# Moving the token tiles of a three-pass matmul within SBUF, with another order of its passes

## The chip, the core and the metric

One core of a Trainium2 chip runs the whole program. The metric is the device time of one execution in microseconds; the kernel before took 1469.27 us (median of 3 runs, 1468.96 to 1470.71).

## The reference

One layer of a decoder for a prompt of 4096 tokens (width 1024) and a sample batch of 64 new tokens. All arithmetic is float32.

```python
h = rmsnorm(x, g_pre)
z = h @ w_in                        # 1024 -> 2816 columns, split among three head groups
out_a = silu(cg) * cb * conv3(cc * ch)                  # gated short convolution, 256 channels
out_b = silu(ag) * window_attention(q, k, v, sink)      # window 128, 8 q heads, 2 kv heads, head dim 64
out_c = silu(mg) * cross_attention(mq, mem_k, mem_v)    # 4 heads, 256 memory tokens
y = concat(out_a, out_b, out_c) @ w_out
out = x + rmsnorm(y, g_post)
```

Beside the two outputs the kernel returns the last keys, values and convolution rows, and the keys and values of the memory.

## The kernel before, in words

**Three passes for float32.** TensorE multiplies float32r operands in one pass. To keep float32 precision each operand is split in two, hi (a rounded copy, made by ScalarE) and lo (the rest, made by VectorE), and a product is hi x hi + hi x lo + lo x hi. In the input projection the weights are the operand that is loaded into the array (128 columns at a time) and the tokens are the operand that is streamed (260 columns at a time).

**The input projection.** The tokens are 8 blocks of 2 x 260 columns, and the 1024 rows of the contraction are two halves of 4 slices (KH) of 128. A weight tile of one product is 128 partitions x 2 x 512: hi and lo of 4 slices x 128 columns. `product` (line 378, its matmul on line 383) runs one product into a PSUM bank: for each slice k the three matmuls (w hi, t hi), (w hi, t lo), (w lo, t hi), twelve in all. Two column blocks of z and two token halves make a 2 x 2 block product, done with 7 products instead of 8 (Strassen's scheme in Winograd's form): `PRODUCTS` names the weight sums (A11 to S4) and the token sums (B11 to T4). Three passes over column groups (`PHASES`: 4, 4 and 3 pairs of column blocks) go through all blocks; within a block the steps p = 0 to 6 take one entry of `PRODUCTS` each, and a step runs that product for its 4 (or 3) pairs q. The first two blocks of the first pass are plain 8-product blocks (`plain_block`), since the weight sums are not there yet. That is 64 + 168 + 224 + 168 = 624 products.

**Token tiles.** Each step needs one hi and one lo tile [128, 4, 260]; `split` (or `x_split` in the plain blocks) makes the next step's while this step's products run. The pool `hp` has two places for hi and two for lo, so steps take the places in turn. Below `hp` on the left stack of SBUF lie the constants, the pool `tiny` for small sums, `wa` with 21 weight tiles, `place` and the pool `hx` of four float32 token tiles; above it lie the z tiles and temporary rows. The fourth pair's weights lie in `wb`, at the right end of SBUF. The weight tiles are reused later for w_out and the split mix of the attention.

**Attention and output projection.** Small pieces of the memory products and of the first attention groups run inside the third pass. Then 32 blocks of 128 tokens follow, one after the other; each runs the output projection of its block (line 1662, 512 streamed columns) between the scores and values of later blocks. `open_attention` lays the pools of this part on the left stack from the end of `place` on, with three unused tiles (gap0, gap1, gap2) between them. Softmax of the cross attention keeps maximum (mx), scaled maximum (nm), sum (den) and reciprocal (rd) in four small tiles with a tag each, three places a tag. The sample batch's attention is done in pieces in blocks 26 to 30 and uses the same tags.

**Order.** The instruction order of TensorE, VectorE, ScalarE, GpSimd and SyncE is the written one in the plain blocks and in the third pass up to the end, and a scheduler's elsewhere. Jobs of VectorE and ScalarE are spread by hand behind the products of each step.

Of the kernel before, what the change touches and what calls it, by code (L numbers as in the profile page):

```python
# [8 lines left out]
F32 = mybir.dt.float32  # L9
F32R = mybir.dt.float32r  # L10
# [5 lines left out]
P = 128  # L16
D = 1024
KT = D // P
KH = KT // 2
# [2 lines left out]
NB = 8  # L22
NT = 4096 + NS
HW = 260
NBLK = NT // (2 * HW)
CT = 256
NCH = 4096 // CT
# [19 lines left out]
def f(ap):  # L47
    return ap.bitcast(F32)
# [3 lines left out]
def hybrid_layer(ctx: ExitStack, tc: tile.TileContext, a: dict):  # L52
# [10 lines left out]
    class InOrder:  # L63
# [6 lines left out]
        def __getattr__(self, name):  # L70
# [4 lines left out]
    V, TE, S, G = (InOrder(engine) for engine in (nc.vector, nc.tensor, nc.scalar, nc.gpsimd))  # L75

    const = ctx.enter_context(tc.tile_pool(name="const", bufs=1))
    tiny = ctx.enter_context(tc.tile_pool(name="tiny", bufs=3))
# [8 lines left out]
    mhalf = const.tile([P, 8], F32, name="mhalf")  # L87
# [5 lines left out]

    diag = const.tile([P, 2 * HW], F32, name="mix_s")
    mix_s = diag[:, : 8 * NS].rearrange("p (k n) -> p k n", n=NS)

    rowd = [tc.dram_tile([2 * HW], F32, name=f"rowd{b}") for b in range(NBLK)]
    hd = [{o: tc.dram_tile([P, KH, HW], F32, name=f"hd{b}_{o}") for o in ("B12", *(o for _, o in PRODUCTS))}
          for b in range(NBLK)]
    sd = {}  # L100
# [9 lines left out]
    pa = ExitStack()  # L110
# [3 lines left out]

    place = ctx.enter_context(tc.tile_pool(name="place", bufs=1)).tile([P, 2, KH, HW], F32, name="place")
    hxp = pa.enter_context(tc.tile_pool(name="hx", bufs=4))
    hp = pa.enter_context(tc.tile_pool(name="hp", bufs=2))
    own = ExitStack()
    kept_z = ExitStack()
    zp, used = {}, {1: [], 2: []}  # L120
# [41 lines left out]
    def z_tile(w, name):  # L162

        pool = zp[w].pop(0)
        used[w].append(pool)
        return pool.tile([P, w, 2, HW], F32, tag="z", name=name)

    def z_done(order):

        for w in zp:  # L170
            zp[w] += [used[w][i] for i in order if i < len(used[w])]
            used[w] = []

    late, late_rows = [], []

# [9 lines left out]
    def store(dst, src):  # L185
        if store_queue[0] is G:
            G.dma_start(dst, src)  # L187
        else:
            late.append(lambda: DMA.dma_start(dst, src))

    def temp(name):
        return tp.tile([P, 2 * HW if 1 in zp else 2 + 2 * HW], F32, tag="t", name=name)
# [80 lines left out]
    def row_load(j):  # L273
        if j < 5 * NBLK:
            g = RG * j - NS
# [11 lines left out]
    def row_step():  # L287

        j = sq[0]
        if j == 5 * NBLK:  # L290
            return
# [48 lines left out]
    def gain_of(o, k):  # L340
        kk = KH * (int(o[1]) - 1) + k
        return gpre[:, kk : kk + 1]
# [25 lines left out]
            store(hd[b][o], ops[o])  # L368

    def split(src, name):  # L370
        hi = hp.tile([P, KH, HW], F32R, tag="hi", name=f"hi{name}")
        lo = hp.tile([P, KH, HW], F32R, tag="lo", name=f"lo{name}")
        S.copy(hi, src)
        V.tensor_tensor(lo, src, f(hi), op=ALU.subtract)
        return hi, lo


    def product(w, h, bank, first=True, last=True):
        i = 0
        for k in range(KH):  # L380
            ks = slice(k * P, (k + 1) * P)
            for l, r in ((w[:, 0, ks], h[0][:, k]), (w[:, 0, ks], h[1][:, k]), (w[:, 1, ks], h[0][:, k])):
                TE.matmul(bank[:, :HW], l, r, start=first and i == 0, stop=last and i == 3 * KH - 1)  # L383
                i += 1

    def evict(p, banks, z1, z2):
# [27 lines left out]
    def finish_parts(b, z, idx, zsi):  # L414

        z = flat(z)
        if b == 0:
            S.copy(zs[:, zsi, :], z[:, :NS])
        if idx == 0 and b == NBLK - 1:
            kl = temp("kl")  # L420
# [9 lines left out]
    def finish_v(b, z):  # L430
        t = temp(f"v{b}")[:, : 2 * HW]
        S.copy(t, flat(z))
        if b == 0:
            S.copy(zs[:, 5, :], t[:, :NS])
        if b == NBLK - 1:
            store(a["o_vp"], t[:, 2 * HW - P :])
# [86 lines left out]
    ws = {}  # L523
# [69 lines left out]
    raw0, zz, pending, h0, kept = {}, {}, {}, {}, {}  # L593

    def x_split(b, o, meanwhile=lambda: None):
        x = xs[0, b][o]
        h0[b, o] = hi, lo = [hp.tile([P, KH, HW], F32R, tag=n, name=f"{n}0_{b}{o}") for n in ("hi", "lo")]
        for k in range(KH):
            if k == 1:
                meanwhile()  # L600
            g = gain_of(o, k)
            S.mul(hi[:, k], x[:, k], g)
            V.scalar_tensor_tensor(lo[:, k], x[:, k], g, f(hi[:, k]), op0=ALU.mult, op1=ALU.subtract)
# [82 lines left out]
    def plain_block(b):  # L686
        banks, zz[b] = {}, [[None, None], [None, None]]
        for s, (wo_, ho, tag) in enumerate(PLAIN):
            flush()
            plain_loads(b, s)  # L690
            jobs, done, adds = plain_jobs(b, s), 0, s % 4 > 1
            row, half = 1 - s % 2, s // 4
            for q in range(4):
                if q % 2 == 0 and not adds:
                    banks[q // 2, tag] = accumulator("xy".index(tag), 2, f"c0_{b}_{q}_{s}")
                product(ws[0, q, wo_], h0[b, ho], banks[q // 2, tag][:, q % 2], not adds, adds)
                if adds and q % 2:
                    if half == 0:
                        zz[b][q // 2][row] = z_tile(2, f"z0_{b}_{q}_{row}")
                    S.copy(zz[b][q // 2][row][:, :, half], banks[q // 2, tag][:, :, :HW])  # L700
                upto = len(jobs) * (q + 1) // 4
                for fn in jobs[done:upto]:
                    fn()
                done = upto
        z_done((0, 1, 2, 3))
# [9 lines left out]
    written_order()  # L715
    x_of(0, 0, "B11", 2)
    first_w("A21")
    S.mul(tiny.tile([P, 8], F32, tag="mx", name="table"), mhalf, 1.0)
    first_w("A11", 0, 1)
    x_of(0, 0, "B21")  # L720

# [244 lines left out]
    last = NBLK - 1  # L966
# [118 lines left out]
    def open_attention():  # L1085

        nonlocal ps, mixp, wp, wl, kp, bq, yp, yq, sp
        own.close()
        psa.close()
        pa.close()  # L1090

        ps = {tag: ctx.enter_context(tc.tile_pool(name=f"ps{tag}", bufs=1, space=bass.MemoryType.PSUM)) for tag in (*range(4), "pv", 4, 5)}
        left = lambda name, bufs=1: att.enter_context(tc.tile_pool(name=name, bufs=bufs))
        bq, kp, third["sm"] = left("bq"), left("kp"), left("sm")
        left("gap0").tile([P, 128], F32, name="gap0")
        yq, mixp, yp0 = left("yq"), left("mixp"), left("yp0")
        left("gap1").tile([P, 64], F32, name="gap1")
        third["skc"], third["sqb"], yp1, wd0 = left("skc"), left("sqb"), left("yp1"), left("wd0")
        left("gap2").tile([P, 48], F32, name="gap2")
        yp = yp0, yp1  # L1100
        sp, wl, wd1 = left("sp"), left("wl"), left("wd1")
        wp = wd0, wd1
# [80 lines left out]
    class Group:  # L1183
# [125 lines left out]
            self.cross_exps(s, hh)  # L1309

        def cross_max(self, s, hh):
            mx, nm, den, rd = (tiny.tile([P, 4], F32, tag=t, name=f"x{t}{self.b}_{hh}")[:, :2] for t in ("mx", "nm", "den", "rd"))
            V.tensor_reduce(mx, s, axis=AX.X, op=ALU.max)
            V.tensor_scalar(nm, mx, -SCALE, None, op0=ALU.mult)
            self.cross_sums[hh] = den, rd, nm
# [156 lines left out]
    def sample_mem(bh):  # L1472
# [6 lines left out]
        p, on, pt = (big[:, i] for i in (8, 9, 10))  # L1479
# [5 lines left out]
        for j in range(2):  # L1485
            for hh in range(2):
                r = slice(hh * 64, hh * 64 + 64)
# [8 lines left out]
        s = psum(3, f"sms{bh}")[:, :256]  # L1496
        for b in range(nb):
            for j in range(2):
                TE.matmul(s[32 * b : 32 * b + 32, :], qb[:, j, b, :], km[:, j, b, :], start=j == 0, stop=j == 1,
                          tile_position=(0, 32 * b))  # L1500
        mx, nm, den, rd = (tiny.tile([P, 4], F32, tag=n, name=f"sm{n}{bh}") for n in ("mx", "nm", "den", "rd"))
        V.tensor_reduce(mx[:, 0:1], s, axis=AX.X, op=ALU.max)
        V.tensor_scalar(nm[:, 0:1], mx[:, 0:1], -SCALE, None, op0=ALU.mult)
        S.activation(p, s, AF.Exp, bias=nm[:, 0:1], scale=SCALE, accum_out=den[:, 0:1])
# [6 lines left out]
        o = psum(2, f"smo{bh}")[:, :256]  # L1511
# [7 lines left out]
        t = psum(3, f"smot{bh}")  # L1519
# [3 lines left out]
        for j in range(2):  # L1523
            for hh in range(2):
                r = slice(hh * 64, hh * 64 + 64)
# [6 lines left out]
    def sample_window():  # L1532
# [6 lines left out]
        for j in range(4):  # L1539
            for kvh in range(2):  # L1540
                r = slice(kvh * 64, kvh * 64 + 64)
# [15 lines left out]
        sm = [sms[i // 2][:, i % 2] for i in range(4)]  # L1557
        for half in range(2):
            s = psum(1 + half, f"sws{half}")
            s3 = s.rearrange("p (h k) -> p h k", h=2)  # L1560
            for i in range(2):
                pr = 2 * half + i
                for b2 in range(2):
                    TE.matmul(s3[b2 * 64 : b2 * 64 + 64, i, 0:P], qb[:, 2 * pr + b2, :], kc[:, 2 * pr + b2, :],
                              start=True, stop=True, tile_position=(0, 64 * b2))
                TE.matmul(s3[:, i, P:192], qb[:, 2 * pr : 2 * pr + 2, :].rearrange("p b c -> p (b c)"), zs[:, 4, :],
                          start=True, stop=True)
            S.copy(sms[half], s3[:, :, 0:192])
        mx = tiny.tile([P, 4], F32, tag="mx", name="swmx")
        for half in range(2):  # L1570
            V.copy_predicated(sms[half], msk[:, 2 * half : 2 * half + 2], neg)
            V.tensor_reduce(mx[:, 2 * half : 2 * half + 2], sms[half], axis=AX.X, op=ALU.max)
        nm = tiny.tile([P, 4], F32, tag="nm", name="swnm")
        V.tensor_scalar(nm, mx, -SCALE, scol[:, 1:2], op0=ALU.mult, op1=ALU.min)
        es = tiny.tile([P, 4], F32, tag="es", name="swes")
        S.activation(es, nm, AF.Exp, bias=scol[:, 0:1])
        den = tiny.tile([P, 4], F32, tag="den", name="swden")
        for i in range(4):
            S.activation(sm[i], sm[i], AF.Exp, bias=nm[:, i : i + 1], scale=SCALE, accum_out=den[:, i : i + 1])
        V.tensor_tensor(den, den, es, op=ALU.add)  # L1580
        rd = tiny.tile([P, 4], F32, tag="rd", name="swrd")
        V.reciprocal(rd, den)
        for i in range(4):
            V.tensor_scalar(sm[i], sm[i], rd[:, i : i + 1], None, op0=ALU.mult)
# [6 lines left out]
        o = psum(4, "swo")  # L1591
# [5 lines left out]
        for j in range(4):  # L1597
            for kvh in range(2):
                r = slice(kvh * 64, kvh * 64 + 64)
# [276 lines left out]
```

## Time and profile before

| | |
|---|---|
| median of the runs | 1469.27 us |
| span of the profiled execution | 1465.5 us |
| the profiled execution's own time | its span, 1465.5 us from first to last instruction; the medians are of whole executions, 3.8 us more |
| TensorE busy | 1453.8 us, 99% |
| TensorE weight loads busy | 1335.6 us, 91% |
| VectorE, ScalarE, GpSimd busy | 82%, 52%, 31% |
| line 383 (`product`) in the chain that ended last | 50% of the span |
| line 1662 (output projection) in that chain | 22% |
| DMA | 337.27 MB, mean 230 GB/s |

Busy time of TensorE says only that some matmul is drawn at every moment: a matmul of 260 columns is drawn 0.28 us long, and the next starts 0.12 us after it. The pace of matmuls is read from the distance of their starts, or from the count of instructions in a window. The times of the profile and of the runs come from different executions.

### The profile page before, as it was taken

What the parts mean: (1) busy time and instruction counts of PE and PEld (TensorE: products, weight loads), DVE (VectorE), ACT (ScalarE), POOL (GpSimd) and SP (SyncE); (2) the same over time, 40 slices, a digit from 0 to 9 for tenths busy, and PEclk for the clock granted to TensorE, in tenths of its full rate; (3) what the DMA queues carried; (4) which work ended last, traced back from release to release, by engine and by line L of the source; (5) the groups of instructions that cost most, each with busy time, mean ns of one, the idle gap of its engine ahead of it and who ended that gap; (6) DMA issues with size and microseconds to landing.
All of it is one profiled execution on the core that took longest, in us unless ns stands there. A gap on an engine that the chain in (4) does not pass through costs nothing.

```text
span 1465.5 us, 30938 instructions
## 1 busy us (share of the span) xinstructions
PE 1453.8 (99%) x11457; PEld 1335.6 (91%) x11457; DVE 1206.9 (82%) x1897; ACT 756.5 (52%) x1869; POOL 448.6 (31%) x622
## 2 busy tenths in 40 slices
PE   9999999999999999999999999999999999999998
PEld 8999999999999999999999999977777777778776
DVE  5869878899998877799668777998889988888853
ACT  5876656566522222234445435665655656665542
POOL 0222223322300000000001222266566565556561
PEclk9999999999999999999999999999999999999999
DMA  9999999886866544475986977999988898998773
GB/s 259 156 272 238 274 257 269 252 299 223 210 241 198 176 146 154 139 257 133 312 287 212 281 253 240 318 271 238 232 237 222 216 248 225 235 238 230 231 213 113
DMA packets 211980, 337.27 MB, mean 230 GB/s; under 512 B 55285, under 2 KB 125941, under 8 KB 211797
## 3 DMA queue, kind: packets, MB, share of 16 engines
q1 hardware_dynamic: 158901, 225.89, 52.1%
q0 software_dynamic: 44144, 78.68, 21.1%
q10 hardware_dynamic: 8784, 30.72, 6.9%
q8 instruction: 91, 1.49, 0.5%
q14 instruction: 60, 0.49, 0.1%
HBM read 192.48 MB, written 110.15 MB: 207 GB/s over the span
## 4 chain that ended last, share of the span: by engine, by line
PE 83%; DMA 7%; issue 3%; SPq 2%; DVE 2%; ACT 2%; POOL 1%; ACTq 0%; POOLq 0%; DVEq 0%
PE c L383 50%; PE y L1662 22%; PE pv L1128 5%; PE ws L1128 3%; SPq L1346 2%; PE xs L1128 1%; DMA mix<-md 1%; DMA x_0B<-in_xt 1%; PE mem_acc L810 1%; DMA md<-th 1%; DMA w<-s 1%; DMA wr_2A<-in_w_in 1%; DMA wr_3S<-sd6S 1%; DMA vd<-v 0%; DMA x_1B<-in_xt 0%
## 5 line engine op out<-in xcount | busy, mean ns | idle before, releaser
L1662 PE MATMUL y<-wo,mh 128*128 128x512 f32 (+1 forms) x1040 | 328.6, 391 | 0.0
L390 DVE TENSOR_TENSOR z<-c,z 128x520 f32<-128x520 f32 (+1 forms) x308 | 193.6, 644 | 71.0 <-PE c L383 69.6
L1662 PEld LDWEIGHTS y<-wo,mh 128*128 128x128 f32 x1040 | 194.2, 188 | 52.2 <-DVE wmx L1287 5.4
L1662 PE MATMUL y<-wo,ml 128*128 128x512 f32 (+1 forms) x520 | 200.9, 386 | 0.0
L1331 POOL TENSOR_SCALAR s<-s,xrd 128x256 f32<-128x256 f32 x124 | 57.9, 479 | 197.0 <-DVE xrd L1326 191.4
L1662 PEld LDWEIGHTS y<-wo,ml 128*128 128x128 f32 x520 | 97.8, 188 | 18.5
L1297 ACT ACTIVATE s<-s,wnm 128x128 f32<-128x128 f32 x256 | 98.7, 387 | 0.0
L756 POOL MEMSET negs<- 128x1 f32 x1 | 0.1, 98 | 285.1 <-DVE w_2A L206 285.1
L1274 ACT COPY s<-ws 128x256 f32<-128x256 f32 x128 | 41.2, 378 | 79.4 <-PE ws L1128 74.2
L1692 POOL TENSOR_TENSOR xr<-yn,xr 128x1024 f32<-128x1024 f32 x29 | 69.3, 2391 | 18.4 <-ACT yn L1691 16.4
L1362 POOL TENSOR_SCALAR_AFFINE_SELECT wd<-w 128x512 f32<-128x512 f32 x64 | 59.1, 924 | 36.3 <-DMA w<-s 18.8
L1670 ACT ACTIVATE y<-y 128x512 f32<-128x512 f32 (+1 forms) x66 | 38.6, 585 | 53.1 <-DVE yn L1669 53.0
L1669 DVE TENSOR_TENSOR yn<-y,gpost 128x512 f32<-128x512 f32 (+1 forms) x66 | 44.7, 678 | 16.2 <-PE y L1662 14.7
L1320 ACT ACTIVATE s<-xs,xnm 128x256 f32<-128x256 f32 x128 | 58.0, 460 | 0.0
L1128 PEld LDWEIGHTS ws<-kst,q 64*128 64x128 f32 x768 | 47.7, 186 | 11.0 <-issue 9.9
L1362 POOL TENSOR_SCALAR_AFFINE_SELECT w<-w 128x512 f32<-128x512 f32 x64 | 56.8, 906 | 2.2
L1278 DVE COPY_PREDICATED s<-wmask,ws 128x256 f32<-128x256 uint8 x124 | 48.0, 441 | 8.5 <-ACT s L1274 6.1
L1128 PE MATMUL ws<-kst,q 64*128 64x256 f32 x768 | 55.0, 288 | 0.0
L392 ACT COPY z<-c 128x520 f32<-128x520 f32 (+1 forms) x44 | 24.3, 554 | 57.5 <-PE c L383 53.4
L296 ACT ACTIVATE nat<-nat 104x1024 f32<-104x1024 f32 x40 | 42.2, 1056 | 18.4 <-DMA nat<-in_x_p 18.4
L1297 ACT ACTIVATION_READ_ACCUMULATOR s<-s,wnm 128x1 f32 x256 | 47.9, 187 | 0.0
L187 POOL DMA_DIRECT2D md<-th x48 | 26.2, 547 | 69.6 <-DVE th L444 34.0
(968 smaller groups left out, 4970.5 us busy)
## 6 DMA issues: line engine op xcount, KB each, us to landing
w<-s SPq DMA_DIRECT2D x456, 64.0 KB
q<-qd POOLq DMA_DIRECT2D x32, 768.0 KB, 6.5
xr<-in_x_p SPq DMA_DIRECT2D x32, 512.0 KB
nat<-in_x_p SPq DMA_DIRECT2D x39, 416.0 KB
o_yp<-xr SPq DMA_DIRECT2D x31, 512.0 KB
md<-th POOLq DMA_DIRECT2D x48, 260.0 KB, 7.2
qd<-zh SPq DMA_DIRECT2D x48, 260.0 KB
qd<-z SPq DMA_DIRECT2D x48, 260.0 KB
```

The source lines that it names most:

```text
L296: S.activation(t[:RG], t[:RG], AF.Square, accum_out=r[:RG, i : i + 1])
L383: TE.matmul(bank[:, :HW], l, r, start=first and i == 0, stop=last and i == 3 * KH - 1)
L390: add = lambda dst, other: V.tensor_tensor(dst, c, other, op=ALU.add)
L1128: ins = TE.matmul(o, w, x, **kw)
L1278: V.copy_predicated(to, squares(third["wmask"]), squares(s3[:, :, 0:P]))
L1297: S.activation(sm[:, h], sm[:, h], AF.Exp, bias=nm[:, h : h + 1], scale=SCALE, accum_out=den[:, h : h + 1])
L1320: S.activation(p[:, i], s[:, i].rearrange("p (a k j) -> p a k j", a=2, k=4), AF.Exp, bias=nm[:, i : i + 1], scale=SCALE, accum_out=den[:, ...
L1331: G.tensor_scalar(p[:, i], p[:, i], rd[:, i : i + 1], 0.5, op0=ALU.mult, op1=ALU.mult)
L1362: G.affine_select(out, src, pattern=[[32 * sign, 2], [0, 8], [sign, 32]], compare_op=op, fill=0.0, base=base * sign, channel_multiplier=-s ...
L1662: TE.matmul(acc, self.hl[l][:, k], wo[k][c0 // 512][:, r, c0 % 512 : c0 % 512 + c1 - c0], start=j == 0, stop=j == passes * KT - 1)
L1669: V.tensor_tensor(yn[:m, c0:c1], acc[:m], gpost[0][:m, c0:c1], op=ALU.mult)
L1692: total = G.tensor_tensor(self.xr, yn, self.xr, op=ALU.add)
```

## The change

Four things.

1. The pool `hp` becomes four pools of one tile each, in the order hi, lo, hi, lo; a tile is 1056 elements a partition instead of 1040, and the tokens begin 12 elements into it. Taken in turn per kind, as before.
2. `product` takes the order of its three matmuls as an argument; as a rule (w hi, t hi), (w lo, t hi), (w hi, t lo). Only the first step of the first block keeps the old order.
3. mx, nm, den and rd are four parts of one tile with 16 elements (tag x4, three places); the tag es has one place. This makes `tiny` 64 elements a partition smaller, as many as the token pools grow.
4. The unused tile gap1 in the attention's stack grows from 64 to 128 elements.

```diff
+HP, HP_AT = 1056, 12
...
-    hp = pa.enter_context(tc.tile_pool(name="hp", bufs=2))
+    hp_pools = [(tag, pa.enter_context(tc.tile_pool(name=f"hp{tag}{n}", bufs=1))) for n in range(2) for tag in ("hi", "lo")]
+
+    def h_tile(tag, name):
+
+        n = next(i for i, (t, _) in enumerate(hp_pools) if t == tag)
+        hp_pools.append(hp_pools.pop(n))
+        t = hp_pools[-1][1].tile([P, HP], F32R, tag=tag, name=name)
+        return t[:, HP_AT : HP_AT + KH * HW].rearrange("p (k n) -> p k n", k=KH)
+
...
+    def fours(name):
+        t = tiny.tile([P, 16], F32, tag="x4", name=name)
+        return [t[:, 4 * i : 4 * i + 4] for i in range(4)]
...
     def split(src, name):
-        hi = hp.tile([P, KH, HW], F32R, tag="hi", name=f"hi{name}")
-        lo = hp.tile([P, KH, HW], F32R, tag="lo", name=f"lo{name}")
+        hi, lo = h_tile("hi", f"hi{name}"), h_tile("lo", f"lo{name}")
...
-    def product(w, h, bank, first=True, last=True):
+    def product(w, h, bank, first=True, last=True, parts=((0, 0), (1, 0), (0, 1))):
         i = 0
         for k in range(KH):
             ks = slice(k * P, (k + 1) * P)
-            for l, r in ((w[:, 0, ks], h[0][:, k]), (w[:, 0, ks], h[1][:, k]), (w[:, 1, ks], h[0][:, k])):
-                TE.matmul(bank[:, :HW], l, r, start=first and i == 0, stop=last and i == 3 * KH - 1)
+            for l, r in parts:
+                TE.matmul(bank[:, :HW], w[:, l, ks], h[r][:, k], start=first and i == 0, stop=last and i == 3 * KH - 1)
                 i += 1
...
-                product(ws[0, q, wo_], h0[b, ho], banks[q // 2, tag][:, q % 2], not adds, adds)
+                product(ws[0, q, wo_], h0[b, ho], banks[q // 2, tag][:, q % 2], not adds, adds,
+                        ((0, 0), (0, 1), (1, 0)) if b + s == 0 else ((0, 0), (1, 0), (0, 1)))
...
-        left("gap1").tile([P, 64], F32, name="gap1")
+        left("gap1").tile([P, 128], F32, name="gap1")
...
-            mx, nm, den, rd = (tiny.tile([P, 4], F32, tag=t, name=f"x{t}{self.b}_{hh}")[:, :2] for t in ("mx", "nm", "den", "rd"))
+            mx, nm, den, rd = (t[:, :2] for t in fours(f"x4{self.b}_{hh}"))
...
-        mx, nm, den, rd = (tiny.tile([P, 4], F32, tag=n, name=f"sm{n}{bh}") for n in ("mx", "nm", "den", "rd"))
+        mx, nm, den, rd = fours(f"sm{bh}")
...
-        mx = tiny.tile([P, 4], F32, tag="mx", name="swmx")
+        mx, nm, den, rd = fours("sw")
...
-        es = tiny.tile([P, 4], F32, tag="es", name="swes")
+        es = tiny.tile([P, 4], F32, tag="es", name="swes", bufs=1)
```

More of the change, by code (lines that the diff above doesn't have):

```diff
@@ L596, in x_split @@
         x = xs[0, b][o]
-        h0[b, o] = hi, lo = [hp.tile([P, KH, HW], F32R, tag=n, name=f"{n}0_{b}{o}") for n in ("hi", "lo")]
+        h0[b, o] = hi, lo = [h_tile(n, f"{n}0_{b}{o}") for n in ("hi", "lo")]
         for k in range(KH):
@@ L717, in hybrid_layer @@
     first_w("A21")
-    S.mul(tiny.tile([P, 8], F32, tag="mx", name="table"), mhalf, 1.0)
+    S.mul(tiny.tile([P, 16], F32, tag="x4", name="table")[:, :8], mhalf, 1.0)
     first_w("A11", 0, 1)
@@ L1572, in sample_window @@
             V.tensor_reduce(mx[:, 2 * half : 2 * half + 2], sms[half], axis=AX.X, op=ALU.max)
-        nm = tiny.tile([P, 4], F32, tag="nm", name="swnm")
         V.tensor_scalar(nm, mx, -SCALE, scol[:, 1:2], op0=ALU.mult, op1=ALU.min)
-        es = tiny.tile([P, 4], F32, tag="es", name="swes")
+        es = tiny.tile([P, 4], F32, tag="es", name="swes", bufs=1)
         S.activation(es, nm, AF.Exp, bias=scol[:, 0:1])
-        den = tiny.tile([P, 4], F32, tag="den", name="swden")
         for i in range(4):
@@ L1580, in sample_window @@
         V.tensor_tensor(den, den, es, op=ALU.add)
-        rd = tiny.tile([P, 4], F32, tag="rd", name="swrd")
         V.reciprocal(rd, den)
```

## The prediction, before the run

> **What bounds the kernel now.** I read the page's first two parts first, then the table of waits of TensorE, then one of windows over the input projection, and last the timeline of TensorE, product by product.
>
> ```profile
> span 1465.5 us, 30938 instructions
> PE 1453.8 (99%) x11457; PEld 1335.6 (91%) x11457; DVE 1206.9 (82%) x1897; ACT 756.5 (52%) x1869; POOL 448.6 (31%) x622
> PEclk9999999999999999999999999999999999999999
> ```
> ```profile
> PE c L383 <- ACT rb L326: 1.1, 1, 1.1
> PE c L383 <- ACT w_0A L202: 0.7, 1, 0.7
> ...
> PE c L383 <- DVE lo_1B L374: 0.3, 1, 0.3
> PE c L383 <- DVE w_0A L206: 0.2, 1, 0.2
> PE c L383 <- DVE w_1A L206: 0.2, 1, 0.2
> ```
>
> TensorE is idle for 1465.5 - 1453.8 = 11.7 us of the whole span, its clock is granted in full, and the waits of the products (line 383) are a few tenths of a us each. No other engine holds it up. So the time is the number of matmuls times their pace, and the pace of line 383 is read from windows (its own instructions alone; the columns are busy time and count of matmuls and of weight loads, granted clock, DMA share, GB/s):
>
> ```profile
> 120.00:200.00 80.00, 80.00 (x669) 80.00 (x668) 1.00 0.98 256
> 200.00:300.00 100.00, 100.00 (x834) 99.97 (x833) 1.00 0.97 277
> 420.00:500.00 80.00, 80.00 (x669) 80.00 (x668) 1.00 0.59 188
> 500.00:650.00 150.00, 150.00 (x1252) 150.00 (x1251) 1.00 0.48 154
> ```
>
> A window also counts the matmuls that reach into it: one is drawn 0.28 us long and they start 0.12 us apart, so about 2.35 too many. 150 us / (1252 - 2.35) is 120.0 ns a matmul, and the busy DMA of the first window (0.98) gives the same as the quiet one of the last (0.48): 80 / (669 - 2.35) = 120.0 ns. Twelve matmuls make a product, **1.440 us on average**; the loops make 64 products in the plain blocks, 168 in the rest of the first pass, 224 and 168 in the other two: 624, or 899 us of the span.
>
> How much of the 120 ns could go at all? The output projection has the same kind of matmul with 512 columns:
>
> ```profile
> 1223.13 0.39 PE L1662 MATMUL y<-wo,ml 128*128 128x512 f32 x1
> 1223.35 0.62 PE L1662 MATMUL y<-wo,mh 128*128 128x512 f32 x2
> 1223.81 0.39 PE L1662 MATMUL y<-wo,ml 128*128 128x512 f32 x1
> ```
>
> Three take 0.68 us, 227 ns each. 252 more columns cost 107 ns, 0.423 ns a column; 260 columns are then 110 ns, and some 10 ns of a product's matmul are not columns. That is what a layout can work on: at most 10 x 7488 = 75 us.
>
> Now the products one by one. The rows are starts, "hi" rows that follow each other are drawn together (x2), so I read from one lo to the next: three matmuls (lo of slice k, hi of slice k, hi of slice k+1).
>
> ```profile
> 521.15 0.29 PE L383 MATMUL c<-lo_4T,w_1S 128*128 128x260 f32 x1
> ...
> 522.60 0.28 PE L383 MATMUL c<-lo_4T,w_2S 128*128 128x260 f32 x1
> ...
> 522.95 0.28 PE L383 MATMUL c<-lo_4T,w_2S 128*128 128x260 f32 x1
> ...
> 523.30 0.28 PE L383 MATMUL c<-lo_4T,w_2S 128*128 128x260 f32 x1
> ...
> 523.66 0.28 PE L383 MATMUL c<-lo_4T,w_2S 128*128 128x260 f32 x1
> ...
> 524.02 0.29 PE L383 MATMUL c<-lo_4T,w_3S 128*128 128x260 f32 x1
> ...
> 525.46 0.28 PE L383 MATMUL c<-lo_4T,w_0S 128*128 128x260 f32 x1
> ...
> 525.82 0.28 PE L383 MATMUL c<-lo_4T,w_0S 128*128 128x260 f32 x1
> ...
> 526.17 0.28 PE L383 MATMUL c<-lo_4T,w_0S 128*128 128x260 f32 x1
> ...
> 526.53 0.28 PE L383 MATMUL c<-lo_4T,w_0S 128*128 128x260 f32 x1
> ...
> 526.88 0.28 PE L383 MATMUL c<-lo_4T,w_1S 128*128 128x260 f32 x1
> ...
> 527.24 0.28 PE L383 MATMUL c<-lo_4T,w_1S 128*128 128x260 f32 x1
> ...
> 527.60 0.29 PE L383 MATMUL c<-lo_4T,w_1S 128*128 128x260 f32 x1
> ...
> 527.98 0.28 PE L383 MATMUL c<-lo_4T,w_1S 128*128 128x260 f32 x1
> ...
> 528.33 0.28 PE L383 MATMUL c<-lo_4T,w_2S 128*128 128x260 f32 x1
> ...
> 529.78 0.28 PE L383 MATMUL c<-lo_4T,w_3S 128*128 128x260 f32 x1
> ...
> 531.23 0.28 PE L383 MATMUL c<-lo_4T,w_0S 128*128 128x260 f32 x1
> ```
>
> Nothing waits here, and still the same twelve matmuls take **1.45, 1.42, 1.44, 1.42, 1.45, 1.45 and 1.45 us**. Up to 525.34 the tokens lie in the first pair of tiles, then in the second. Counting the pools' sizes from the weights' pool on (each weight tile is 1024 elements a partition, so all are alike modulo 64; then place with 2080, the x tiles with 4 x 1040, the token tiles with 1040 each), the first pair begins 32 (hi) and 0 (lo) elements behind the weights modulo 64, the second 48 and 16; each slice k adds 260, which is 4. So before, hi reads at 32 to 44 and 48 to 60, lo at 0 to 12 and 16 to 28. In the second pair the stretch from slice 2 to 3 (lo 24, hi 56, hi 60) takes 0.38 us in one product (527.60 to 527.98, a bump) and 0.36 in the one before it (526.17 to 526.53): where the streams lie matters, and so does how the product was entered.
>
> **The change part by part.**
>
> *Places.* Four pools of 1056 elements (32 modulo 64) and a start 12 into each put both hi tiles at 32 + 12 = 44 and both lo tiles at 12; slices read at hi 44, 48, 52, 56 and lo 12, 16, 20, 24. All of these occur before, so each slice has a row: hi 44 with lo 12 is the last stretch of the first pair, 523.66 to 524.02, 0.36 us; hi 48 with lo 16 the second pair's first, 0.36; hi 52 with lo 20 its second, 0.35 (525.82 to 526.17) or 0.36 (527.24 to 527.60); hi 56 with lo 24 its third, 0.36 or 0.38. Together **1.43 us a product if the last runs as in the short product, 1.46 if it runs as in the longer one**. The stretches are not the same sets as after (each ends in a hi of the next slice), so this is an estimate from the nearest rows.
>
> *Order.* (w hi, t hi), (w hi, t lo), (w lo, t hi) becomes (hi, hi), (lo, hi), (hi, lo). As many matmuls and weight loads. hi is streamed twice running, which line 383 never does before within a slice; line 1662 does so with its streamed operand, and its three matmuls keep 0.68 us. As a price of its own I take 0, and bound it by the shortest and longest stretch above: 0.35 and 0.38 against the mean 0.360 are -0.010 and +0.020 us for three matmuls, four times a product, 624 times: -25 to +50 us. The row it is nearest to is the short product, where the same slices run without a bump.
>
> *Which pattern.* Both pairs of tiles now look alike modulo 64, so there is one pattern instead of two that alternate step by step. Both old pairs reach 1.42 us in one product of four, by different offsets; the others lie at 1.44 to 1.45. I take the middle between the short products and the sum of the rows, 1.425 us: 624 x (1.440 - 1.425) = **-9.4 us**.
>
> *Waits.* A late lo now has one more matmul (0.12 us) in front of it: -0.1 us of the 0.3 in the table. A late low weight has one less: +0.1 us each at worst, but the two rows with such waits (w_0A, w_1A) lie in the first step, where the edit keeps the old order. Together 0. Behind a waiting matmul stand only TensorE's own.
>
> *Small sums in one tile.* mx, nm, den and rd of a group become parts of one tile, three in rotation as before. They are used in a row (maximum, scaled, exponentials, reciprocal, weights), so the parts don't wait for each other. New is that the maximum on VectorE waits until GpSimd has used rd three allocations earlier.
>
> ```profile
> 948.79 0.68 DVE L1313 TENSOR_REDUCE xmx<-xs 128x2 f32<-128x512 f32 x1
> ...
> 954.28 1.84 POOL L1331 TENSOR_SCALAR s<-s,xrd 128x256 f32<-128x256 f32 x4 [11.96 <-DVE xrd L1326]
> ...
> 962.38 0.68 DVE L1313 TENSOR_REDUCE xmx<-xs 128x2 f32<-128x512 f32 x1
> ```
>
> These are a group and the second maximum of the next: GpSimd is done at 956.12, the maximum comes at 962.38, 6.3 us later. Cost 0. If GpSimd ran 6.3 us late, VectorE would wait with the band copies and mix products queued behind it, and TensorE with the next group's scores; each us of that would cost at most 31 us over the groups.
>
> *Memory.* The sums give up 64 elements, the token pools take 64, the gap in the attention's stack grows from 64 to 128: pools behind it stay, those before it move by 64, and all offsets modulo 64 with them. Weights 3 lie in the pool at the right end, which by the same count is 64 off the other weights modulo 128; their product and that of weights 1 take 1.44 and 1.45 us with the first pair, 1.45 both with the second. So 64 costs nothing that these rows can tell, and the attention stays.
>
> **Sum**: -9.4 us on 1465.5 gives a span of 1456.1; the runs lie 1469.27 - 1465.5 = 3.8 us above the span, so **1460 us**.
>
> **The rivals.**
>
> *The bump comes in every product.* Place: slice 3, hi 56 and lo 24, exactly the stretch of 0.38 us. Before, every second step moves to the other pair and starts anew (the first product at 525.34 is a short one); after, nothing in the offsets changes from step to step, and a product could stay locked at 1.45. Cost: 624 x (1.45 - 1.44) = +6 us, 1475; by the 1.46 of the rows +12, 1482. It decides if the bump at slice 3 survives the new order. For it: three of the four products of the second pair have it. Against it: the order that leads into slice 3 is another.
>
> *Nothing happens.* Pace follows from entry alone, not from places or order, and the mix of 1.42 and 1.45 stays: 1469. For it: the same places give both. [...]
>
> *The conflict goes away.* Every stretch runs at the best seen, 0.35 us: 1.40 us a product, -25 us, 1444. For it: 0.35 occurs in both pairs. Against it: no product has four of them.
>
> *The gain is eaten by DMA.* Between 120 and 300 us DMA is busy at 0.97 to 0.98; of 899 us these are 180, so at most 2 us of 9.4 are lost: 1462, inside the forecast.
>
> **How the numbers follow.** Forecast (1.415 to 1.435 us a product, 1453 to 1466) 0.38; conflict gone 0.17; nothing 0.18; bump in every product 0.27. What this kernel's measurement can tell from no change is about 0.2%, 2.9 us. Forecast and conflict gone are faster: 0.55; the null is 0.18; slower, with the bump, 0.27. The range leaves out the upper end of the bump's rival and the lower end of the best: 1444 to 1477.
>
> **What would show it.** In the timeline of the changed kernel a step's four products should take about 1.42 to 1.43 us each, in both pairs alike, and the windows at 500 us show x1260 or more in 150 us. Stretches of 0.37 or more at slice 3 would show the bump's rival; a mix of 1.42 and 1.45 the null. The output projection must keep 0.68 us for three; if the attention is longer, the shared sums or the shift by 64 were not free. Wrong would be a change of the span that the products don't carry.

## The result, and the profile after

The changed kernel takes **1458.76 us** (median of 6 runs, 1454.94 to 1462.21) against 1468.62 us of the kernel before (6 runs, 1467.42 to 1470.71): **0.9937 of its time, 95% interval 0.9920 to 0.9953**. The forecast was 1460 us, and 1456.1 us for the span; the profiled span is 1455.4 us.

The first two lines of the page after, and the waits of TensorE after (in all, times, longest):

```profile
span 1455.4 us, 30944 instructions
PE 1443.5 (99%) x11457; PEld 1325.2 (91%) x11457; DVE 1205.9 (83%) x1897; ACT 757.7 (52%) x1869; POOL 453.3 (31%) x622
```
```profile
PE pv L1141 <- ACT y L1680: 1.6, 2, 1.0
PE idle L737 <- POOL mhalf L89: 1.5, 1, 1.5
PE c L395 <- ACT w_0A L215: 0.8, 1, 0.8
PE c L395 <- DVE w_0S L219: 0.8, 1, 0.8
PE c L395 <- DVE w_0A L219: 0.2, 1, 0.2
```

TensorE is idle for 11.9 us, before 11.7; its busy time fell by 10.3 us, the span by 10.1. So no wait went away: as many matmuls follow each other more closely. The windows of the products' line (395 now) after, columns as in the prediction:

```profile
200.00:300.00 100.00, 99.94 (x849) 99.74 (x848) 1.00 0.98 278
500.00:650.00 150.00, 150.00 (x1264) 150.00 (x1263) 1.00 0.53 176
```

Before there were 834 and 1252 matmuls in these. Less the 2.35 that reach in, a product of twelve takes 1.417 us in the first window (a short wait of 0.06 us in it) and 1.427 in the second, before 1.443 and 1.440. Where the time came from shows in the last eviction of the projection and the first and last start of the output projection's matmuls, after and then before:

```profile
L402 DVE TENSOR_TENSOR z<-c,z x308: 411/694/710, 112.2 to 929.8; 128x520 f32<-128x520 f32 x146, 128x260 f32<-128x260 f32 x8
...
L1672 PE MATMUL y<-wo,mh x1040: 277/389/504, 926.9 to 1448.9; 128*128 128x512 f32 x168, 128*128 128x256 f32 x6
```
```profile
L390 DVE TENSOR_TENSOR z<-c,z x308: 409/693/701, 116.0 to 941.4; 128x520 f32<-128x520 f32 x146, 128x260 f32<-128x260 f32 x8
...
L1662 PE MATMUL y<-wo,mh x1040: 278/389/504, 938.7 to 1459.0; 128*128 128x512 f32 x168, 128*128 128x256 f32 x6
```

The projection ends 11.6 us earlier; the part behind it is 1.7 us longer (522.0 us from the first to the last start of the output projection, before 520.3).

The timeline of TensorE after, in three places: rows at the first lo of consecutive products in the first, second and third pass.

```profile
200.58 0.28 PE L395 MATMUL c<-lo_4T,w_3S 128*128 128x260 f32 x1
...
202.00 0.28 PE L395 MATMUL c<-lo_4T,w_0S 128*128 128x260 f32 x1
...
203.41 0.28 PE L395 MATMUL c<-lo_4T,w_1S 128*128 128x260 f32 x1
...
500.73 0.28 PE L395 MATMUL c<-lo_4B,w_1A 128*128 128x260 f32 x1
...
502.15 0.28 PE L395 MATMUL c<-lo_4B,w_2A 128*128 128x260 f32 x1
...
503.58 0.28 PE L395 MATMUL c<-lo_4B,w_3A 128*128 128x260 f32 x1
...
505.01 0.28 PE L395 MATMUL c<-lo_4B,w_0A 128*128 128x260 f32 x1
...
676.45 0.28 PE L395 MATMUL c<-lo_0T,w_0S 128*128 128x260 f32 x1
...
677.88 0.28 PE L395 MATMUL c<-lo_0T,w_1S 128*128 128x260 f32 x1
...
679.33 0.28 PE L395 MATMUL c<-lo_0T,w_2S 128*128 128x260 f32 x1
...
680.76 0.28 PE L395 MATMUL c<-lo_0B,w_0S 128*128 128x260 f32 x1
```

Products take 1.41 to 1.42 us in the first pass, 1.43 in the second, 1.43 to 1.45 early in the third. By the starts in the trace, which the timeline rounds to 10 ns, these are **three lengths, 1413, 1427 and 1440 ns, each repeated to within 1 ns** over many products, with both pairs of tiles alike; of 588 products with no wait and no other matmul in them, 253 take 1413 ns, 237 take 1427 and 77 take 1440 (each to 2 ns). Before, lengths from 1420 to 1453 ns alternated. The first change of length comes here:

```profile
343.42 0.40 PE L395 MATMUL c<-hi_0B,w_0A 128*128 128x260 f32 x2
343.66 0.40 PE L395 MATMUL c<-hi_0B,w_2A 128*128 128x260 f32 x2
343.90 0.28 PE L395 MATMUL c<-lo_0B,w_0A 128*128 128x260 f32 x1
```

The scheduler put two matmuls of another product between the second and third of this one, and from the next products on 1.413 us has become 1.427. That lasted 13 products. Two later breaks changed the length again:

```profile
366.25 0.28 PE L395 MATMUL c<-hi_0B,w_0S 128*128 128x260 f32 x1
367.34 0.39 PE L395 MATMUL c<-hi_0B,w_0S 128*128 128x260 f32 x1 [0.81 <-DVE w_0S L219]
...
402.18 0.39 PE L395 MATMUL c<-lo_1T,w_0S 128*128 128x260 f32 x1
402.41 0.40 PE L395 MATMUL c<-hi_1T,w_0S 128*128 128x260 f32 x2
```

At 366 us TensorE waited for a weight, and the products behind it take 1.413 us again. At 402.41 us a matmul starts 0.23 us after the one before it, about 0.1 us late, and then 185 products in a row take 1.427 us, up to 667 us. So most of the second pass took its length behind the late matmul at 402 us, not behind the two matmuls at 343 us.

### The profile page after: what moved, and what is told of

Same layout as the page of the kernel before. It is cut to its first block, busy times and chain, and to the rows that moved or that the text cites. A ratio compares the mean times of both kernels' runs of the same rounds, so it can differ in the third digit from the quotient of the medians.

```text
span 1455.4 us, 30944 instructions
## 1 busy us (share of the span) xinstructions
PE 1443.5 (99%) x11457; PEld 1325.2 (91%) x11457; DVE 1205.9 (83%) x1897; ACT 757.7 (52%) x1869; POOL 453.3 (31%) x622
## 4 chain that ended last, share of the span: by engine, by line
PE 89%; DMA 3%; issue 3%; DVE 2%; SPq 1%; POOL 1%; ACT 1%; ACTq 0%; DVEq 0%; POOLq 0%
PE c L395 56%; PE y L1672 22%; PE pv L1141 5%; PE ws L1141 3%; PE xs L1141 1%; PE mem_acc L823 1%; SPq L1359 1%; DMA mix<-md 1%; DMA nat<-in_x_p 1%; DMA vd<-v 0%; DMA w<-s 0%; DMA wr_0S<-sd0S 0%; DMA wr_1A<-in_w_in 0%; DMA o_yp<-xr 0%; POOL md L200 0%
## 5 line engine op out<-in xcount | busy, mean ns | idle before, releaser
L1344 POOL TENSOR_SCALAR s<-s,x 128x256 f32<-128x256 f32 x124 | 58.3, 482 | 200.1 <-DVE x L1339 194.4
L1375 POOL TENSOR_SCALAR_AFFINE_SELECT wd<-w 128x512 f32<-128x512 f32 x64 | 62.1, 970 | 34.9 <-DMA w<-s 24.4
L1333 ACT ACTIVATE s<-xs,x 128x256 f32<-128x256 f32 x128 | 58.2, 463 | 0.0
L1679 DVE TENSOR_TENSOR yn<-y,gpost 128x512 f32<-128x512 f32 (+1 forms) x66 | 44.8, 678 | 14.6 <-PE y L1672 13.3
```

Of the source, the lines that this page charges most:

```text
L1333: S.activation(p[:, i], s[:, i].rearrange("p (a k j) -> p a k j", a=2, k=4), AF.Exp, bias=nm[:, i : i + 1], scale=SCALE, accum_out=den[:, ...
L1344: G.tensor_scalar(p[:, i], p[:, i], rd[:, i : i + 1], 0.5, op0=ALU.mult, op1=ALU.mult)
L1375: G.affine_select(out, src, pattern=[[32 * sign, 2], [0, 8], [sign, 32]], compare_op=op, fill=0.0, base=base * sign, channel_multiplier=-s ...
L1679: V.tensor_tensor(yn[:m, c0:c1], acc[:m], gpost[0][:m, c0:c1], op=ALU.mult)
```

## The experiments

The prediction had argued that the offsets of the tokens behind the weights, modulo 64 elements, set the pace together with the way a product is entered, and that the order of the three matmuls is free. The other possibilities: the order does it, or neither does. Places are written hi/lo: 44/12 says that hi begins 44 and lo 12 elements behind the weights, modulo 64. They are counted from the sizes of the pools; the traces show no addresses. For every kernel one line is shown, its products' window from 500 to 650 us in the second pass (before x1252, 1.440 us a product; one matmul more is 1.1 ns less); lengths in ns are from the starts in the trace.

### The new order alone

```diff
 # the kernel before, plus
+    def product(w, h, bank, first=True, last=True, parts=((0, 0), (1, 0), (0, 1))):
...
+            for l, r in parts:
+                TE.matmul(bank[:, :HW], w[:, l, ks], h[r][:, k], start=first and i == 0, stop=last and i == 3 * KH - 1)
...
```

> The kernel before with the new order of the three matmuls alone; token tiles stay at 32/0 and 48/16 in turn. If the places decide (offsets 44 and 12 with their slices): no change, ratio 0.998 to 1.002, products of 1.42 to 1.45 us that alternate between the two pairs, slice 3 of the second pair with its bump. If the order decides (the hi tokens streamed twice running): ratio 0.993 to 0.995, products of 1.41 to 1.43 us in both pairs. If both are needed: a part of it, above 0.996.

```profile
500.00:650.00 150.00, 150.00 (x1261) 150.00 (x1260) 1.00 0.50 165
```

1462.3 us, ratio 0.9963 (0.9951 to 0.9975): what was expected if both parts are needed. Products are 1.430 us in this window; those with hi at 32 take 1436 ns in the mean (before 1439), those with hi at 48 take 1427 (before 1443). So the order is not free, contrary to the prediction: at 48/16 it is worth 15 ns a product, at 32/0 two or three. It also takes the bump away: before, 209 of 268 products at 48/16 have a stretch of 0.37 us or more from the lo of slice 2 to the lo of slice 3; with the new order, at the same places, none of 269 has one.

### The new places alone

```diff
 # the changed kernel
-    def product(w, h, bank, first=True, last=True, parts=((0, 0), (1, 0), (0, 1))):
+    def product(w, h, bank, first=True, last=True, parts=((0, 0), (0, 1), (1, 0))):
...
-                        ((0, 0), (0, 1), (1, 0)) if b + s == 0 else ((0, 0), (1, 0), (0, 1)))
+                        ((0, 0), (0, 1), (1, 0)))
```

> The changed kernel with the old order (w hi, t hi), (w hi, t lo), (w lo, t hi); token tiles at 44 and 12. If the places decide: ratio 0.993 to 0.995 and products of 1.41 to 1.43 us. If the order decides: ratio 0.998 to 1.004. If what counts is that both pairs of tiles lie alike, products repeat to within 1 ns until TensorE next has to wait, and the ratio follows from the length in which they settle (1.413 us: 0.988; 1.427: 0.994; 1.440: 1.000).

```profile
500.00:650.00 150.00, 150.00 (x1264) 150.00 (x1263) 1.00 0.49 162
```

1459.71 us, ratio 0.9946 (0.9926 to 0.9966). Products take 1427 ns in all three passes (571 of 589), as in the changed kernel's second pass. The places alone give most of the gain; the order then adds products of 1413 ns, but also of 1440. The times of the kernels with and without the new order (0.9937 and 0.9946) can't be told apart; their products can. Whether the two parts add up is not shown: as times they give 0.0054 + 0.0037 apart and 0.0063 together, and the intervals leave both open.

### The shared sums alone

```diff
 # the changed kernel with hp, split, x_split and the order of the kernel before
...
+    hp = pa.enter_context(tc.tile_pool(name="hp", bufs=2))
...
```

> The small sums in shared tiles and the larger gap1 alone; token tiles and order as before (all pools from wa to the z tiles move down by 64 elements). Every theory: ratio 0.998 to 1.002, attention blocks 15.9 us apart as before. If the shared sums make VectorE wait for GpSimd, the attention is longer by 1 us or more and the ratio above 1.001.

```profile
500.00:650.00 150.00, 150.00 (x1252) 150.00 (x1251) 1.00 0.48 154
```

1466.47 us, ratio 0.9992 (0.9983 to 1.0002): no change that can be told, and the same count of matmuls. The pools from `wa` to the z tiles moved by 64 elements here, weights 3 at the right end did not, and the same lengths came back, with weights 3 too: 64 elements made no difference here, 1.440 us a product in this window before and after.

### The changed kernel once more

> The changed kernel once more. If the length of a product is fixed by the addresses alone, the same lengths come at the same places: 1.413 us up to 343 us, 1.427 up to 690 us, 1.440 in the last pass. If a wait of TensorE lets it settle anew, the three lengths come again, but their stretches differ, and the span lies anywhere between 1453 and 1461 us.

```profile
500.00:650.00 150.00, 150.00 (x1276) 150.00 (x1276) 1.00 0.54 178
```

One run, 1455.69 us. In the second pass, where the first profile had 1427 ns, this execution has 1413. The program and its addresses are the same, so **the length isn't fixed by them alone: 1427 ns in one execution, 1413 in the other**. 224 products of 13.3 ns are 3.0 us; the second pass is 2.8 us shorter than in the first profile. Behind the break by the two matmuls of another product both executions take 1.427 us for 13 or 14 products, and behind the next waits 1.413 us again. They part between 396 and 405 us, where other matmuls come late: the first profile goes on at 1.427 us for 185 products, this one, after three products of 1.427 us, at 1.413 us for 184.

### Four other places

```diff
-HP, HP_AT = 1056, 12
+HP, HP_AT = 1056, 0      # hi 32, lo 0;   16: hi 48, lo 16;   8: hi 40, lo 8
 # and for hi 12, lo 44:
-    hp_pools = [... for n in range(2) for tag in ("hi", "lo")]
+    hp_pools = [... for n in range(2) for tag in ("lo", "hi")]
```

> The changed kernel with the tokens at the start of the tiles: both pairs at hi 32, lo 0, slices 4 further each. If each offset has its own cost, the products take what they took at 32/0 with the new order while the pairs alternated, 1.436 us (span about 1463). If alike pairs let the products settle, all take the same length, a step of 13.3 ns on the ladder 1.413, 1.427, 1.440, and stay there until TensorE waits; spans of 1449 to 1466.

```profile
500.00:650.00 150.00, 150.00 (x1255) 150.00 (x1254) 1.00 0.47 153
```

> The changed kernel with the tokens 8 elements into the tiles: both pairs at hi 40, lo 8; slices hi 40 to 52 and lo 8 to 20. Of the offsets of 44/12 it drops slice 56/24, which had the bump of the kernel before, and adds 40/8. If the bump's offset costs: below 1.413 us a product, span under 1449. If the products settle on the ladder: one of 1.400, 1.413, 1.427, 1.440 and uniform. If the offset has no say beyond being alike: the same lengths as at 44/12.

```profile
500.00:650.00 150.00, 150.00 (x1261) 150.00 (x1261) 1.00 0.51 168
```

> The changed kernel with the tokens 16 elements into the tiles: both pairs at hi 48, lo 16. If each offset has its own cost: 1.427 us a product, as at 48/16 with the new order while the pairs alternated (span about 1458). If alike pairs settle: uniform lengths on the ladder 1.413, 1.427, 1.440.

```profile
500.00:650.00 150.00, 150.00 (x1264) 150.00 (x1263) 1.00 0.51 168
```

> The changed kernel with hi and lo tiles exchanged: hi at 12, lo at 44, both pairs alike. If only the set of offsets counts: lengths as at 44/12, 1.413 to 1.440 us. If the twice streamed operand's offset counts more: another length, since two of three matmuls then read at 12 to 24; by the offsets' own rows of the kernel before (12: 117.9 ns, 16: 119.1, 20: 119.5, 24: 126.2) 1.45 us.

```profile
500.00:650.00 150.00, 150.00 (x1246) 150.00 (x1246) 1.00 0.46 149
```

One run each: 1468.25, 1461.27, 1458.51 and 1471.35 us, beside one run of the kernel before with 1467.61; 1.437, 1.430, 1.427 and 1.447 us a product. At 32/0, 48/16 and 12/44 that is what was expected if each offset has its own cost; at 40/8 none of the three expectations was met. Each place has its own mean and keeps it, to 1 ns, through all passes; at 32/0 products of 1430 and 1443 ns alternate, at 40/8 products of 1427 and 1433. The means of 32/0 and 48/16, 1437 and 1427 ns, are what these places took while they alternated step by step in the kernel with the new order alone (1436 and 1427 ns): **in the mean, changing from pair to pair cost 1 ns at most here; the mean went with the place.** At 40/8, without slice 56/24, products take 1430 ns, at 48/16, which has it, 1427: what was costly in that slice before isn't its offset as such.

### Tokens and weights 0 to 2 moved by 8 elements, weights 3 left in place

```diff
-        es = tiny.tile([P, 4], F32, tag="es", name="swes", bufs=1)
+        es = mss
-        left("gap1").tile([P, 128], F32, name="gap1")
+        left("gap1").tile([P, 136], F32, name="gap1")
```

> The changed kernel with the left stack of SBUF 8 elements lower from the weights' pool on (the tile es is dropped, its place is taken by a constant that is no longer read; gap1 grows by 8): weights 0 to 2 and the tokens move together, weights 3, at the right end, stay. Tokens lie 44 and 12 behind weights 0 to 2 as before, and 36 and 4 behind weights 3. If the distance of tokens to weights sets the pace: products of weights 0 to 2 still on 1.413, 1.427 or 1.440 us once settled, those of weights 3 of another length (third pass, without weights 3, as in the changed kernel). If the tokens' own address sets it: all products alike, between those of 44/12 and 32/0, also in the third pass.

The window, and the starts of consecutive products in the timeline:

```profile
500.00:650.00 150.00, 150.00 (x1267) 150.00 (x1266) 1.00 0.51 169
```
```profile
500.28 0.40 PE L395 MATMUL c<-hi_3T,w_3A 128*128 128x260 f32 x2
...
501.73 0.40 PE L395 MATMUL c<-hi_4B,w_0A 128*128 128x260 f32 x2
...
503.15 0.40 PE L395 MATMUL c<-hi_4B,w_1A 128*128 128x260 f32 x2
...
504.56 0.40 PE L395 MATMUL c<-hi_4B,w_2A 128*128 128x260 f32 x2
...
505.98 0.40 PE L395 MATMUL c<-hi_4B,w_3A 128*128 128x260 f32 x2
...
507.42 0.40 PE L395 MATMUL c<-hi_4B,w_0A 128*128 128x260 f32 x2
```

One run, 1458.21 us (the kernel before 1467.26, median of 13). Products take 1.42, 1.41 and 1.42 us with weights 0 to 2 and 1.45 and 1.44 with weights 3, which alone didn't move; in the second pass 1417 ns in the mean against 1444. In the third pass, which has no weights 3, the lengths are 1413, 1427 and 1440 again. The expectation was met in part: weights 0 to 2 are as fast as before, but beside products of weights 3 their lengths are 1419, 1413 and 1417 ns, of which only one is among the three. Neither the tokens' own address nor the weights' own decided here: the tokens moved, and weights 0 to 2 kept their pace; weights 3 stayed, and lost it. So in this run **the pace went with the distance of the tokens from the weights, not with the tokens' own address** (unless two opposite effects of the same size cancel, which was not tried); eight elements of that distance were worth some 27 ns a product (1444 against 1417).

### Half a step, another entry, another way

```diff
 # hi 46, lo 14
-HP, HP_AT = 1056, 12
+HP, HP_AT = 1056, 14
 # lo first, at 44/12
-    def product(w, h, bank, first=True, last=True, parts=((0, 0), (1, 0), (0, 1))):
+    def product(w, h, bank, first=True, last=True, parts=((0, 1), (0, 0), (1, 0))):
...
-                        ((0, 0), (0, 1), (1, 0)) if b + s == 0 else ((0, 0), (1, 0), (0, 1)))
+                        ((0, 0), (0, 1), (1, 0)) if b + s == 0 else ((0, 1), (0, 0), (1, 0)))
 # slices downwards, at 44/12
-        for k in range(KH):
+        for k in range(KH)[::-1]:
```

> The changed kernel with the tokens 14 elements into the tiles: hi 46, lo 14, half a step between 44/12 and 48/16. If only whole 4-element steps count: the lengths of 44/12 (1.413 to 1.440 us) or 48/16 (1.427). If single elements count: a length of its own, between 1.400 and 1.440 us.

```profile
500.00:650.00 150.00, 150.00 (x1224) 150.00 (x1224) 1.00 0.44 139
```

> The changed kernel with the order (w hi, t lo), (w hi, t hi), (w lo, t hi): the same round of lo, hi, hi, entered at another point, so that only the step from product to product differs. If the round alone decides: 1.413, 1.427 and 1.440 us appear again, span 1453 to 1461 us. If the step between products decides which is kept: one length throughout; 1.413 everywhere would give 1449 to 1452 us, 1.440 everywhere 1466.

```profile
500.00:650.00 150.00, 150.00 (x1250) 150.00 (x1248) 1.00 0.48 154
```

> The changed kernel with the slices from 3 to 0: tokens read at hi 56, 52, 48, 44 and lo 24, 20, 16, 12. If an offset has a cost of its own, the sequence doesn't matter: 1.413 to 1.440 us. If the way from slice to slice counts (260 elements back instead of on): another length, 1.400 to 1.450 us.

```profile
500.00:650.00 150.00, 150.00 (x1241) 150.00 (x1240) 1.00 0.45 146
```

1485.91 us, ratio 1.0128 (1.0113 to 1.0143); 1468.43 us, ratio 1.0011 (1.0000 to 1.0022); 1474.65 us, ratio 1.0052 (1.0037 to 1.0067): 1.473, 1.443 and 1.453 us a product in the mean, the same in all passes; with lo first, products of 1437 and 1449 ns alternate. None met its expectation. The one start that is not a multiple of four elements makes the longest products of all kernels here. With lo first, the operands are the same at the same places, but after hi of slice k comes lo of slice k+1 instead of k, and the gain is gone; with the slices downwards it turns into a loss. So in these kernels an offset had no cost of its own that could be added up: the same offsets took 1.413 to 1.440 us in the changed kernel, 1.427 with the old order, 1.443 with lo first and 1.453 with the slices downwards, where only the sequence of the stretches differs.

## Why the prediction was right, point by point

**What bounds the kernel.** Right. The time is the number of matmuls times their pace: in every kernel the change of the span is, to within 3.5 us, 624 times the change of the mean product; that is close for the large changes, while at 32/0 the products say -2.5 us and the span says +1.0. The largest: half a step, 624 x (1473.1 - 1440.8) ns = 20.2 us, the span grew by 19.6.

**Places.** The rows of the kernel before gave 1.43 us without the bump and 1.46 with it for the offsets of 44/12. With the old order, which those rows have, 1.427 was measured: the estimate held. The bump at slice 3 is gone, and either part alone removes it: with the new order none of the products at 48/16 has it, and at 44/12 with the old order none has it either, from the lo of slice 2 to the lo of slice 3. The matmuls at 56, 56 and 24 take 120, 118 and 117 ns in the first pass after; before, those at 56 and then 24 took 125 and 128 ns in three of four products. But adding offsets was no method: it gave 1.45 for 12/44 (1.447 measured), and would have given 1.41 to 1.44 for the slices downwards (1.453).

**Order.** The term failed: a price of 0 was taken, from three matmuls of line 1662 that keep 0.68 us. At 44/12 the order moves the product from 1427 ns to a mean of 1423 in one profile and 1417 in the other, which over 624 products is -2.6 and -6.0 us, inside the bounds that the prediction gave; at 48/16 it moves it from 1443 to 1427, and lo first at 44/12 makes it 1443. The three matmuls of line 1662 have other operands at other places and 512 columns, so they are no price for this order here.

**Which pattern.** Half right. One pattern for both pairs came, but not one length: the forecast of 1.425 us is met by a mean (1423 ns) over products of 1.413, 1.427 and 1.440 us, of which only the middle one lies in its 1.415 to 1.435. The sum came out because they lie on both sides: 624 x (1440.8 - 1422.9) ns is 11.2 us against the 9.4 forecast. That it came so close is partly luck, since the same program had a mean of 1417 ns in the next profile.

**Waits, shared sums, memory.** Right as far as these runs tell: TensorE is idle for 11.9 us, before 11.7, the sums alone are 0.9992 (0.9983 to 1.0002), and the two pairs of tiles, which after lie 64 apart modulo 128, take the same length to 1 ns, with all four weights. The 1.7 us that the attention is longer in the profile aren't explained. By the same starts of the trace, the kernel with the new order alone, which has neither shared sums nor the shift, is 2.2 us longer behind the last product than the kernel before, so the 1.7 us need not come from the sums or the shift. The other kernels, all of which have both, are 0.9 to 3.3 us longer there than the one profile before; what makes the difference stays open.

**The rivals.** *Nothing happens* fell: in one execution, products of the second pass take 1417 ns with weights 0 to 2 and 1444 with weights 3, which differ by 8 elements in their distance from the tokens. *The bump in every product* fell: none of the 588 has a stretch of 0.37 us at slice 3. *The conflict goes away* (1.40 us) was not seen in any kernel. *DMA* did not eat the gain: in the window from 200 to 300 us its share is 0.98, and the products there are the shorter ones, 1.417 us against 1.427 in the window from 500 to 650 us.

**What stays open.** Why 44/12 allows three lengths 13.3 ns apart, what chooses among them when the sequence is broken, and where the longer products lose their time. The six runs of the changed kernel lie further apart (7.3 us) than the six before beside them (3.3 us), but fifteen later runs of the kernel before lie 6.3 us apart, so a wider spread is not shown. Other lengths make 2.8 us in the second pass between the two profiles; what they do to the other runs was not tried.

## What to carry to other kernels

When TensorE is busy throughout and nothing waits, compare the same instructions with each other: here 1.5 ns between the starts of equal matmuls (17.9 ns a product, 1440.8 to 1422.9) were 11.2 us, nearly as much as all the idle time of TensorE (11.7 us). The place of the streamed operand relative to the loaded one (8 elements of it were worth 27 ns a product here, 64 nothing) and which stretch follows which (1.413 to 1.453 us at the same offsets) are then parameters to be measured together; rows of another sequence did not add up to them here (for the slices downwards 1.41 to 1.44 us, measured 1.453). One profile may show one of several lengths of the same program (1427 and 1413 ns in the second pass here), so such a change is judged by several runs.

## What the runs showed of the hardware that was not expected

- A stream of equal matmuls, 260 columns each with a new load of weights, kept a length per product to 1 ns for 185 products in a row, and at 44/12 with the new order there were three such lengths: 1413, 1427 and 1440 ns. Behind a matmul that came 0.1 us late (at 402 us), and behind two matmuls of another product in between (at 343 us), 1413 had become 1427.
- The one start tried that is two elements off a multiple of four made the longest products: 1473 ns at 46/14, against 1413 to 1440 at 44/12 and 1427 at 48/16.
- Eight elements of distance from the weights counted here, 64 made no difference: when the tokens moved by 64 elements and weights 3 did not, all lengths stayed (1441 ns a product on average, before and after); when the tokens moved by 8 and weights 3 did not, products of weights 3 took 1444 ns and the others 1417.
